# A pair of column blocks with two groups of seven products: the left block's last k group ahead of both groups in place of between them

## The chip, the cores and the metric

The kernel runs on one core of one Trainium2 chip. The metric is device time in microseconds (us) of one execution. TensorE (PE in the profile) multiplies, VectorE (DVE) and ScalarE (ACT) work element by element, GpSimd (POOL) and SyncE (SP) issue transfers here.

## The reference, cut to what matters

A decoder trunk of two layers on 256 tokens of width 2048, all in float32. Each layer has a mixer (Mamba-2 in the first, attention with forget gates in the second) and then a gated feed-forward part:

```python
def swiglu(h, w_gate_up, w_down):
    g, u = jnp.split(h @ w_gate_up, 2, axis=-1)
    return (jax.nn.silu(g) * u) @ w_down
```

The change touches `h @ w_gate_up`: 256 x 2048 by 2048 x 11264, once in each layer.

## The kernel before

**Products.** Every weight matrix is streamed once through the chip in units of 128 x 1024 numbers (512 KB: two slices of k by 512 columns). Each unit is split in two parts of lower precision: ACT casts it (`whi`, line 273), DVE subtracts the cast from the original (`wlo`, line 279). The activations are held split in the same way (`xT`, or `xS` for sums of them). A product is then the three matmuls xh*hi, xh*lo and xl*hi, added up in PSUM. An ordinary unit takes 12 matmuls (lines 554 to 556), since there are two blocks of 128 tokens.

**Pairs.** Columns are worked on in blocks of 512. `pair` takes two blocks at once: in the gate/up stage (`ffn_up`) the left one is a block of the gate matrix, the right one the same block of the up matrix. k is cut in four k groups (0 to 3). For the k groups in `crossed` the left and right weights, two by two, are multiplied by a scheme with seven products in place of eight, called f, d, c, a, e, g, b in the order in which they run (`Cross.ORDER`). Such a group (`Group`) loads five units: f, d and g are units of the weights, c and a are sums of two units, made in DRAM in advance (`next_sum`: a copy issued by SP, then an adding transfer issued by POOL). Each product takes six matmuls (lines 466 to 469). Products e and b need further sums of weights: behind the split of c, DVE adds unit d to unit c in place (line 428), and that is what e splits; behind the split of e it adds unit g, and that is what b splits.

In 9 of the 11 pairs of each layer's gate/up stage `crossed` is (1, 2), so two groups stand in one pair, and `adjacent` is true; the first and the last pair have one group. No other stage has neighbouring k groups in `crossed`, so the change concerns 18 pairs. In this text the units of a pair are L0a, L0b (left block, k group 0), R0a, R0b (right block), L3a, L3b, R3a, R3b (k group 3), the products of the first group f to b, and those of the second f' to b'.

**Who runs ahead of whom.** `stream` writes all work out in order. ACT and DVE split four pieces (units or products) ahead of the matmuls (`SPL`), into pools of four `whi` and four `wlo` buffers: the split of a piece can begin when PE is done with the piece four places before it. Units are loaded by SP into a pool of six `wraw` buffers (`RAW`); a load waits until the buffer's earlier unit has been read for the last time. What follows a pair's matmuls (silu, gating, turning the result for the next stage) is written by `Flow` between the pieces. The turning of the last pair's result takes eight matmuls against an identity matrix (line 588) and two DVE instructions (`xT<-mis`); they stand behind R0b of the next pair.

Of the kernel before, what the change touches and what calls it, by code (L numbers as in the profile page):

```python
# [232 lines left out]
def kernel(ctx: ExitStack, tc: tile.TileContext, xT_d, x_d, cols_d, rows_d, wdt_d, win_d,  # L233
# [86 lines left out]
    def halves(b, kg, src, ks):  # L320
        w = src.rearrange("p (k n) -> p k n", n=NB)
        return [Unit(b, kg, w[:, 2 * i:2 * i + 2], NB, ks[i]) for i in range(2)]
# [14 lines left out]
    def pair(xs, sources, done, fills, crossed, parts):  # L337


        both = [Block(xs, d, f) for d, f in zip(done, fills)]  # L340
        x = Cross(*both, parts)
        order, rights = [], []
        adjacent = len(crossed) > 1 and crossed[-1] == crossed[-2] + 1
        for kg in range(len(xs)):
            us = [halves(b, kg, src[kg], ([0, 2], [1, 3])) for b, src in zip(both, sources)]
            if kg in crossed:
                if not (adjacent and kg == crossed[-1]):
                    order += rights
                    rights = []
                (b11, b21), (b12, b22) = us  # L350
                c, a = Sum(b22.src, b12.src), Sum(b22.src, b21.src)
                sums.extend((c, a))
                first = {"f": b12, "d": b21, "c": Unit(None, kg, c, NB, [1, 3]),
                         "a": Unit(None, kg, a, NB, [1, 3]), "g": b11}
                order.append(Group(x, first, xs[kg], kg == crossed[0], kg == crossed[-1]))
            else:
                for b, u in zip(both, us):
                    b.units += u
                order += us[0]
                rights += us[1]  # L360
        if adjacent:

            n = next(i for i in range(len(order) - 1, 0, -1) if isinstance(order[i], Group))
            both[0].after = order.pop(n)
            order.append(both[0].after)
        blocks.append(order + rights)

    def next_sum():
# [327 lines left out]
    def out_stage(xs, w_d, wcol, crossed, summed=()):  # L696

        ss = const.tile([P, NT, 4], F32, name=nm("ss"))
        nxt = [Slot(j in summed) for j in range(4)]
        r = [None]  # L700

        def done(j):
            def run(ps):
                for t in range(NT):
                    hb = h[:, t, j * NB:(j + 1) * NB]
                    yield tt(hb, hb, ps[t])
                yield EVAC
                nxt[j].task = spawn(take(j), flow.mid)
            return run

        def take(j):
            yield SYNC
            yield from h_slot(nxt[j], j, wcol)
            for t in range(NT):
                sumsq(h[:, t, j * NB:(j + 1) * NB], ss[:, t, j:j + 1])
                yield A(0.6)
            if j == 3:
                tot = tiny(NT, "tot")
                nc.vector.tensor_reduce(out=tot, in_=ss, axis=AX.X, op=ALU.add)
                r[0] = rsqrt_of(tot, DM, NT)  # L720

        for j in (0, 2):
            pair(xs, w_d[j:j + 2], (done(j), done(j + 1)), nxt[j:j + 2], crossed, parts_to_h(j))
        return nxt, r

    def ffn_up(xs, r, gu_d, summed):
# [41 lines left out]
        for nb in range(NFB):  # L768
            x = [None]

            def took(y, x=x):
                x[0] = y
                return parts(y)

            pair(xs, gu_d[2 * nb:2 * nb + 2], (lambda ps, x=x: gate(x[0], ps), lambda ps, x=x, nb=nb: up(x[0], ps, nb)),
                 (None, acts[nb]), (1, 2) if 0 < nb < NFB - 1 else (2,), took)
# [515 lines left out]
    for j in (0, 2):  # L1292
        pair(act1, dn1_d[j:j + 2], (final(j), final(j + 1)), (None, None), DN1, parts_to_h(j))
# [104 lines left out]
```

## Time and profile before

| what | us |
|---|---|
| median of 3 runs | 2487.26 (2486.73 to 2488.52) |
| the profiled execution, own time | 2488.41 |
| its span, first to last instruction | 2486.6 |
| PE busy | 2477.7 |
| DVE busy | 1973.2 |
| ACT busy | 1435.0 |

The profiled execution's time is 1.15 above the median of the runs shown, inside their spread; 1.8 of it lies outside the span. Instructions overlap a little in the records, and a matmul's record (0.39) is longer than the distance to the next one (0.23), so a busy PE is read by the starts of its matmuls.

### The profile page before, as it was taken

Reading aid. Unit: us, or ns where it says so; the run is one execution under the profiler, and the core shown is the slowest. Engines: PE = TensorE matmul, PEld = TensorE weight load, DVE = VectorE, ACT = ScalarE, POOL = GpSimd, SP = SyncE. Lnnn points to the kernel's source line nnn. Section 1 sums busy time; section 2 is a strip of 40 time slices with the busy share of each in tenths; the row PEclk is TensorE's granted clock in tenths of the full one; section 3 lists DMA queues with packets and bytes.
Section 4 is the critical chain, followed back from the end, with each engine's and each line's share of the span. In section 5 each row is a group of like instructions: output and inputs, shape, how many; then the busy total and the mean of one; then the engine's idle time right before and its main releaser. Section 6 shows DMA issues by size and latency. Waiting matters only on the chain.

```text
span 2486.6 us, 31889 instructions
## 1 busy us (share of the span) xinstructions
PE 2477.7 (100%) x11446; PEld 2056.6 (83%) x11446; DVE 1973.2 (79%) x2557; ACT 1435.0 (58%) x1807; POOL 133.6 (5%) x168
## 2 busy tenths in 40 slices
PE   9999999999999999999999999999999999999999
PEld 8888888888888888888888888888888888888787
DVE  6677777778688999997766657678889999988867
ACT  6665566555555656564545556565565656555544
POOL 0000000000000000000000011010000000000000
PEclk9999999999999999999999999999999999999999
DMA  7887868778887988887888888676889898988765
GB/s 253 261 251 230 256 212 253 220 236 276 276 257 258 296 260 296 258 293 248 263 271 256 260 238 249 208 221 209 262 254 299 285 300 271 286 251 260 244 226 184
DMA packets 173599, 633.34 MB, mean 255 GB/s; under 512 B 19424, under 2 KB 20592, under 8 KB 171904
## 3 DMA queue, kind: packets, MB, share of 16 engines
q1 hardware_dynamic: 154656, 559.50, 64.4%
q0 software_dynamic: 18208, 71.39, 15.8%
q8 instruction: 90, 1.47, 0.2%
q14 instruction: 69, 0.57, 0.1%
q10 hardware_dynamic: 576, 0.40, 0.1%
HBM read 629.04 MB, written 123.81 MB: 303 GB/s over the span
## 4 chain that ended last, share of the span: by engine, by line
PE 98%; DVE 1%; ACT 1%; issue 0%; DMA 0%; ACTq 0%; DVEq 0%
PE acc L554 24%; PE acc L556 24%; PE acc L555 23%; PE mis L466 4%; PE mis L469 4%; PE mis L467 4%; PE acc L467 3%; PE acc L469 3%; PE acc L466 3%; PE mis L588 1%; PE mis L1027 1%; DVE wlo L279 1%; PE mis L897 0%; ACT whi L273 0%; DVE wraw L428 0%; PE mis L1033 0%
## 5 line engine op out<-in xcount | busy, mean ns | idle before, releaser
L279 DVE TENSOR_TENSOR wlo<-wraw,whi 128x1024 fp32r<-128x1024 f32 (+1 forms) x959 | 1147.5, 1219 | 306.3 <-ACT whi L273 298.0
L273 ACT CAST whi<-wraw 128x1024 fp32r<-128x1024 f32 (+1 forms) x962 | 989.1, 1049 | 671.6 <-PE acc L556 456.3
L554 PE MATMUL acc<-whi,xT 128*128 128x512 f32 x2496 | 982.0, 393 | 0.4 <-ACT whi L273 0.3
L556 PE MATMUL acc<-whi,xT 128*128 128x512 f32 x2496 | 973.1, 390 | 0.0
L555 PE MATMUL acc<-wlo,xT 128*128 128x512 f32 x2496 | 972.7, 390 | 0.0
L556 PEld LDWEIGHTS acc<-whi,xT 128*128 128x128 f32 x2496 | 469.0, 188 | 98.6
L554 PEld LDWEIGHTS acc<-whi,xT 128*128 128x128 f32 x2496 | 469.3, 188 | 97.3 <-issue 1.6
L555 PEld LDWEIGHTS acc<-wlo,xT 128*128 128x128 f32 x2496 | 469.4, 188 | 96.1 <-DVE wlo L279 1.2
L281 DVE SCALAR_TENSOR_TENSOR wlo<-wraw,cols,whi 128x512 fp32r<-128x512 f32 x192 | 134.7, 748 | 72.0 <-ACT whi L275 71.6
L275 ACT ACTIVATE whi<-wraw,cols 128x512 fp32r<-128x512 f32 x192 | 127.6, 717 | 72.2 <-PE acc L556 55.1
L428 DVE TENSOR_TENSOR wraw<-wraw,wraw 128x1024 f32<-128x1024 f32 x116 | 142.1, 1225 | 4.0
L467 PE MATMUL mis<-wlo,xS 128*128 128x512 f32 x348 | 135.5, 389 | 0.4 <-DVE wlo L279 0.4
L466 PE MATMUL mis<-whi,xS 128*128 128x512 f32 x348 | 135.4, 389 | 0.0
L469 PE MATMUL mis<-whi,xS 128*128 128x512 f32 x348 | 135.4, 389 | 0.0
L377 POOL DMA_DIRECT2D wsum<-in_gu_dram x80 | 66.3, 829 | 1026.9 <-DMA wsum<-in_gu_dram 1011.0
L467 PE MATMUL acc<-wlo,xT 128*128 128x512 f32 x224 | 87.6, 391 | 1.8 <-DVE wlo L279 1.8
L466 PE MATMUL acc<-whi,xT 128*128 128x512 f32 x224 | 87.2, 389 | 0.0
L469 PE MATMUL acc<-whi,xT 128*128 128x512 f32 x224 | 87.2, 389 | 0.0
L467 PEld LDWEIGHTS mis<-wlo,xS 128*128 128x128 f32 x348 | 65.3, 188 | 14.5 <-DVE wlo L279 0.9
L466 PEld LDWEIGHTS mis<-whi,xS 128*128 128x128 f32 x348 | 65.3, 188 | 13.6
L469 PEld LDWEIGHTS mis<-whi,xS 128*128 128x128 f32 x348 | 65.3, 188 | 13.5
L273 ACT CAST xT<-mis 128x512 fp32r<-128x512 f32 x52 | 27.9, 589 | 54.5 <-PE mis L588 52.4
(250 smaller groups left out, 2109.2 us busy)
## 6 DMA issues: line engine op xcount, KB each, us to landing
wraw<-in_gu_dram SPq DMA_DIRECT2D x312, 512.0 KB, 6.4
wraw<-in_dn_dram SPq DMA_DIRECT2D x164, 512.0 KB, 5.6
wraw<-in_win_dram SPq DMA_DIRECT2D x159, 512.0 KB, 5.9
wraw<-wsum SPq DMA_DIRECT2D x116, 512.0 KB, 5.9
wsum<-in_gu_dram SPq DMA_DIRECT2D x80, 512.0 KB, 6.8
wsum<-in_gu_dram POOLq DMA_DIRECT2D x80, 512.0 KB, 8.8
wraw<-in_wout_dram SPq DMA_DIRECT2D x60, 512.0 KB, 6.3
wraw<-in_wq_dram SPq DMA_DIRECT2D x32, 512.0 KB, 5.8
```

What stands on the lines that cost most here:

```text
L273: nc.scalar.copy(out=hi, in_=src)
L275: nc.scalar.activation(hi, src, AF.Copy, scale=scal)
L279: nc.vector.tensor_tensor(out=lo, in0=src, in1=hi.bitcast(F32), op=ALU.subtract)
L281: nc.vector.scalar_tensor_tensor(out=lo, in0=src, scalar=scal, in1=hi.bitcast(F32), op0=ALU.mult, op1=ALU.subtract)
L377: nc.gpsimd.dma_start(out=old.tile, in_=old.other, accum_op=ALU.add)
L428: nc.vector.tensor_tensor(out=us[out].raw, in0=us[in0].raw, in1=us[in1].raw, op=ALU.add)
L466: nc.tensor.matmul(ps, lhsT=xh, rhs=hi[:, p, :], start=group.first and p == 0 and name not in own, stop=False)
L467: nc.tensor.matmul(ps, lhsT=xh, rhs=lo[:, p, :], start=False, stop=False)
L469: nc.tensor.matmul(ps, lhsT=xl, rhs=hi[:, p, :], start=False, stop=stop and p == 1)
L554: nc.tensor.matmul(b.ps[t], lhsT=xh, rhs=hi[:, j, :], start=u is b.units[0] and ks[j] == 0, stop=False)
L555: nc.tensor.matmul(b.ps[t], lhsT=xh, rhs=lo[:, j, :], start=False, stop=False)
L556: nc.tensor.matmul(b.ps[t], lhsT=xl, rhs=hi[:, j, :], start=False, stop=last and j == len(ks) - 1)
```

## The change

In `pair`, when the two groups are neighbours: before, the last group was taken out and put behind the left block's last k group, which gave L0 R0 *group* L3 *group'* R3. Now all units come first and both groups behind them: L0 R0 L3 *group* *group'* R3. `after`, the group that ends the left block, is the second group in both.

```diff
         if adjacent:
 
-            n = next(i for i in range(len(order) - 1, 0, -1) if isinstance(order[i], Group))
-            both[0].after = order.pop(n)
-            order.append(both[0].after)
+            order = [u for u in order if isinstance(u, Unit)] + [u for u in order if isinstance(u, Group)]
+            both[0].after = order[-1]
         blocks.append(order + rights)
```

The new file has one line less, so lines behind it have a number lower by one.

On PE the change shows where the first group ends. Before, in a pair of the first layer, the second half of product b (`acc_7761`) and the first half unit of L3a behind it:

```order
L466 MATMUL acc_7761<-whi_7881,xT_5282 128x512
L467 MATMUL acc_7761<-wlo_7882,xT_5282 128x512
L469 MATMUL acc_7761<-whi_7881,xT_5282 128x512
L554 MATMUL acc_7760<-whi_7901,xT_6099 128x512
L555 MATMUL acc_7760<-wlo_7902,xT_6099 128x512
L556 MATMUL acc_7760<-whi_7901,xT_6099 128x512
```

In the changed kernel the same place of the same pair, with the first half of f' behind b:

```order
L465 MATMUL acc_7761<-whi_7917,xT_5282 128x512
L466 MATMUL acc_7761<-wlo_7918,xT_5282 128x512
L468 MATMUL acc_7761<-whi_7917,xT_5282 128x512
L465 MATMUL acc_7802<-whi_7937,xS_5991 128x512
L466 MATMUL acc_7802<-wlo_7938,xS_5991 128x512
L468 MATMUL acc_7802<-whi_7937,xS_5991 128x512
```

The 24 matmuls of L3a and L3b have moved from between the groups to ahead of the first one.

On DVE, before, from product e on: e, the sum for b, g, b, L3a, L3b, f', d', c', the sum for e', a' (`wlo` is a split, `wraw<-wraw,wraw` a sum of weights):

```order
L279 TENSOR_TENSOR wlo_7859<-wraw_7704,whi_7858 128x1024
L428 TENSOR_TENSOR wraw_7704<-wraw_7704,wraw_7738 128x1024
L279 TENSOR_TENSOR wlo_7871<-wraw_7738,whi_7870 128x1024
L279 TENSOR_TENSOR wlo_7882<-wraw_7704,whi_7881 128x1024
L279 TENSOR_TENSOR wlo_7902<-wraw_7758,whi_7901 128x1024
L279 TENSOR_TENSOR wlo_7915<-wraw_7779,whi_7914 128x1024
L279 TENSOR_TENSOR wlo_7927<-wraw_7819,whi_7926 128x1024
L279 TENSOR_TENSOR wlo_7939<-wraw_7885,whi_7938 128x1024
L279 TENSOR_TENSOR wlo_7955<-wraw_7887,whi_7954 128x1024
L428 TENSOR_TENSOR wraw_7887<-wraw_7887,wraw_7885 128x1024
L279 TENSOR_TENSOR wlo_7974<-wraw_7892,whi_7973 128x1024
```

In the changed kernel from the same product on: e, the sum for b, g, b, f', d', c', the sum for e', a', e', the sum for b', g':

```order
L279 TENSOR_TENSOR wlo_7895<-wraw_7738,whi_7894 128x1024
L427 TENSOR_TENSOR wraw_7738<-wraw_7738,wraw_7779 128x1024
L279 TENSOR_TENSOR wlo_7907<-wraw_7779,whi_7906 128x1024
L279 TENSOR_TENSOR wlo_7918<-wraw_7738,whi_7917 128x1024
L279 TENSOR_TENSOR wlo_7938<-wraw_7800,whi_7937 128x1024
L279 TENSOR_TENSOR wlo_7951<-wraw_7820,whi_7950 128x1024
L279 TENSOR_TENSOR wlo_7961<-wraw_7870,whi_7960 128x1024
L427 TENSOR_TENSOR wraw_7870<-wraw_7870,wraw_7820 128x1024
L279 TENSOR_TENSOR wlo_7974<-wraw_7924,whi_7973 128x1024
L279 TENSOR_TENSOR wlo_7984<-wraw_7870,whi_7983 128x1024
L427 TENSOR_TENSOR wraw_7870<-wraw_7870,wraw_7926 128x1024
L279 TENSOR_TENSOR wlo_7995<-wraw_7926,whi_7994 128x1024
```

The two splits of L3 have gone from between b and f' to ahead of f, and nothing else stands between e and g'.

## Rows read from the trace of the kernel before

**Rows 1.** The page: busy time by engine, and the chain that ended last.

```profile
PE 2477.7 (100%) x11446; PEld 2056.6 (83%) x11446; DVE 1973.2 (79%) x2557; ACT 1435.0 (58%) x1807; POOL 133.6 (5%) x168
...
PE 98%; DVE 1%; ACT 1%; issue 0%; DMA 0%; ACTq 0%; DVEq 0%
```

**Rows 2.** Busy us by stretch: nine pairs in each layer; clock, DMA share, GB/s.

```profile
733.00:1109.00 376.00, 376.00 (x1697) 312.04 (x1696) 341.70 (x340) 224.83 (x241) 14.67 (x18) 1.00 0.85 277
1825.00:2201.00 376.00, 376.00 (x1697) 312.06 (x1696) 341.67 (x341) 226.75 (x245) 17.10 (x21) 1.00 0.90 286
```

**Rows 3.** Waits of PE, whole span: total us, times, longest.

```profile
PE acc L467 <- DVE wlo L279: 1.8, 3, 0.6
```

**Rows 4.** Timeline of PE: f', d', and R3a of one pair begin.

```profile
851.61 0.39 PE L466 MATMUL acc<-whi,xS 128*128 128x512 f32 x1
851.84 0.39 PE L467 MATMUL acc<-wlo,xS 128*128 128x512 f32 x1
...
852.75 0.39 PE L469 MATMUL acc<-whi,xS 128*128 128x512 f32 x1
...
861.13 0.39 PE L554 MATMUL acc<-whi,xT 128*128 128x512 f32 x1
```

**Rows 5.** Timeline of DVE, same pair, and six splits of the next one.

```profile
850.18 1.22 DVE L279 TENSOR_TENSOR wlo<-wraw,whi 128x1024 fp32r<-128x1024 f32 x1 [1.14 <-ACT whi L273]
851.44 1.23 DVE L428 TENSOR_TENSOR wraw<-wraw,wraw 128x1024 f32<-128x1024 f32 x1
...
854.30 1.23 DVE L279 TENSOR_TENSOR wlo<-wraw,whi 128x1024 fp32r<-128x1024 f32 x1 [0.18 <-ACT whi L273]
855.56 1.23 DVE L428 TENSOR_TENSOR wraw<-wraw,wraw 128x1024 f32<-128x1024 f32 x1
856.71 3.64 DVE L279 TENSOR_TENSOR wlo<-wraw,whi 128x1024 fp32r<-128x1024 f32 x3
...
861.59 2.35 DVE L279 TENSOR_TENSOR wlo<-wraw,whi 128x1024 fp32r<-128x1024 f32 x2
...
883.70 7.04 DVE L279 TENSOR_TENSOR wlo<-wraw,whi 128x1024 fp32r<-128x1024 f32 x6
```

**Rows 6.** Timeline of ACT in the same second group.

```profile
853.22 1.06 ACT L273 CAST whi<-wraw 128x1024 fp32r<-128x1024 f32 x1 [0.35 <-PE acc L469]
854.58 1.06 ACT L273 CAST whi<-wraw 128x1024 fp32r<-128x1024 f32 x1 [0.30 <-PE mis L469]
856.90 2.00 ACT L273 CAST whi<-wraw 128x1024 fp32r<-128x1024 f32 x2 [1.27 <-DVE wraw L428]
```

**Rows 7.** Timeline of DVE and PE in the group of the layer's first pair.

```profile
720.57 1.23 DVE L279 TENSOR_TENSOR wlo<-wraw,whi 128x1024 fp32r<-128x1024 f32 x1 [0.50 <-ACT whi L273]
721.83 1.22 DVE L428 TENSOR_TENSOR wraw<-wraw,wraw 128x1024 f32<-128x1024 f32 x1
722.97 2.50 DVE L279 TENSOR_TENSOR wlo<-wraw,whi 128x1024 fp32r<-128x1024 f32 x2
725.51 1.23 DVE L428 TENSOR_TENSOR wraw<-wraw,wraw 128x1024 f32<-128x1024 f32 x1
...
726.97 0.39 PE L466 MATMUL acc<-whi,xT 128*128 128x512 f32 x1
727.92 0.50 PE L467 MATMUL acc<-wlo,xT 128*128 128x512 f32 x1 [0.56 <-DVE wlo L279]
...
728.26 0.39 PE L469 MATMUL acc<-whi,xT 128*128 128x512 f32 x1
```

**Rows 8.** Loads (line 397) from issue to landing: 852:855, 877:882, 1825:2201.

```profile
DMA to landing us min/median/max: 6.2/6.3/6.4
...
DMA to landing us min/median/max: 3.9/4.0/4.1
...
DMA to landing us min/median/max: 3.3/6.5/9.8
```

## The prediction

> **What bounds the kernel now.** I read the page first: PE is busy for 2477.7 us of 2486.6, and the chain that ended last runs over PE for 98% of the span [rows 1]. So time is saved only where PE stands still, and lost wherever something new makes it stand still. Then I cut out the nine pairs with two groups of each layer. PE is busy for 376.00 of 376.00 us in both stretches, at the full clock, and DVE for 341.7, which is 91% [rows 2]. Over the whole span PE waited only three times for a split, 1.8 us in all [rows 3]. In these 18 pairs there is nothing to win on PE, and DVE, which makes half of each split, is close behind it.
>
> The timelines of one pair show how close. PE starts f' at 851.61 and R3a, 42 matmuls later, at 861.13 [rows 4]: 9.52 us for a group, 1.36 for a product, 0.227 for a matmul. DVE has nine instructions in a group, seven splits and two sums, each of 1.22 us; where nothing is waited for it starts the next one 1.13 after the last (two splits take 2.35) [rows 5]. Nine times 1.13 is 10.2, and the waits for ACT between them come on top. Inside a group DVE is slower than PE. With an ordinary unit it is the other way round: 1.13 against the 2.72 of 12 matmuls. So a group uses up DVE's lead, and ordinary units give it back.
>
> The lead cannot be large. In the second group the cast of e starts at 853.22, released by PE [rows 6]: the last matmul of f began at 852.75 and takes 0.39 [rows 4]. That is the pool of four buffers: e takes that of f. DVE follows at 854.30 [rows 5].
>
> **The change, worked out.** No instruction is added or taken away; what counts is the distance. Before, L3a and L3b, 5.44 us of PE's time, lay between the groups and took 2.3 us of DVE's, so DVE won 3 us back. Now f' comes straight behind b. The rows of the second group before serve for the first group after, because both follow L3a and L3b and have the same instructions in the same order. I count on that pair's clock, f starting at 851.61.
>
> The first group does not wait. Its tightest product is g: its split starts at 856.71 and ends at 857.93 [rows 5]; the split's low part is read by the second matmul of g, at 851.61 + 5 x 1.36 + 0.23 = 858.64. There is 0.71 to spare.
>
> Next DVE goes straight on. The run of three splits from 856.71 is g, b and the piece behind it [rows 5], now f': it starts 3.64 - 1.22 = 2.42 after g, at 859.13. Then d' and c' at 1.13 each: 860.26 and 861.39. ACT is not in the way: b and f' are cast by 858.90 [rows 6], d' follows at once, and c' needs PE to be done with g, at 858.41 + 5 x 0.227 + 0.39 = 859.93, so its cast ends at about 861.0.
>
> From c' on the trace has the very sequence, in the only group of the layer's first pair, where DVE was late for another reason: split of c at 720.57, sum, a, e (whose cast waits for the sum), sum, g, and PE's second matmul of g starts at 727.92 after a wait on DVE [rows 7]. That is 7.35 us. So g' can go on at 861.39 + 7.35 = 868.74. Without a wait PE would be there at 851.61 + 12 x 1.36 + 0.23 = 868.16. It stands still for 0.58. The matmul behind the awaited one came 0.34 after it in place of 0.23 [rows 7], another 0.11. Together 0.69 us for each pair.
>
> What is late next is little. b' is split 1.28 after g' (its cast waits for the sum; the run of three is 1.28 + 1.14 + 1.22) while PE comes to its second matmul 1.47 after that of g', so it is in time by some 0.2. R3a and R3b then give DVE 2.72 each, and the work behind a pair (silu, gating, the turning) is written into that stretch and the next units as before. The turning's two DVE instructions now stand between the splits of f and d, in the time of L3a, which covers them.
>
> The loads move too. SP's queue has the same issues in another order, and the sums needed for the first group are asked for two units later, which helps. In the closest place, unit c' takes the buffer that the first sum of the group sets free, at 851.44 + 1.23 = 852.67 [rows 5]. Its cast may begin as late as 861.39 - 1.06 = 860.33 without cost, an allowance of 7.7 us. Two loads issued in just that place took 6.2 and 6.4, two issued into a quieter queue 3.9 and 4.1, and the stretch in layer 2 has a median of 6.5 and a longest of 9.8 [rows 8]. Unit g' goes out when g is split, at 857.93, and is first needed by the sum for b', at 861.39 + (725.51 - 720.57) = 866.33: 8.4 us. I take both as hidden, cost nothing; the upper bound is 9.8 - 7.7 = 2.1 us in a pair.
>
> The sum is 18 x 0.69 = 12.4 us, all of it added. The profiled execution took 2488.41, so 2500.8 beside it; against the median of the runs, 2487.26, this gives 2499.7, and I say 2500.
>
> One rule speaks for more. The row of six splits in a run takes 7.04 [rows 5], where six times 1.22 is 7.32: DVE's records overlap. The Trainium skill, page "VectorE: DVE Perf Modes", section "The DRAIN you can't avoid", has it that the next Vector instruction does not start before the pipeline of the last one is empty; read strictly, with the records as the time in the pipeline, there is no such overlap. By that rule the spacing is the record. In the run from e to g' six starts follow at about 1.13 to 1.14 (g, f', d', c', a', g'), and 0.085 more for each makes 0.51 more per pair, 21.6 us in all. I go by the row.
>
> **The rivals.**
> - *DVE is in time after all (not slower).* The place is g' again. The wait is 0.58 over a run of twelve DVE instructions from e to g'; if each took 0.03 less, or c' were split 0.3 earlier, less than 5 us would be lost in all, and from 0.58 on nothing. For it: the margin is small against 14.4 us of counted work. Against it: every step is a measured distance, and the start of the run is tied to PE by the buffer of f, so no lead can be saved up. Time 2487 to 2492.
> - *Loads become the bound.* Two groups back to back use ten units in 19 us, and the sums' copies and adding transfers share the DMA engines, which are 85 to 90% busy [rows 2]. If a third of the pairs paid the upper bound of 2.1, that is 6 x 2.1 = 12.6 more: 2512. Against it: the six ordinary units ahead of the groups now stand together, and their loads come at PE's pace of 2.72, so the queue should be short when c' is asked for.
> - *DVE's spacing stretches to its records.* 18 x (0.69 + 0.51) = 21.6: 2509. The row of six speaks against it.
> - *Faster.* PE would have to stand still somewhere that the change closes. All its waits on splits are 1.8 us [rows 3], and none lies in the stretches of the 18 pairs [rows 2]. Some 2485 at best, and only by an effect on another stage.
>
> **How the numbers follow.** My forecast 0.72; in time after all 0.12; loads 0.08; stretched spacing 0.05; faster 0.03. A change of 0.2%, 5 us, is about what a measurement of this kernel can tell from none. My own case has a small tail below 0.28 per pair, so: faster 0.04, same 0.13, slower 0.83. My own case alone runs from 2494 (0.4 per pair) to 2505 (1.0 per pair). The range goes on to 2491 at the low end, which takes in a part of the first rival, and to 2509 at the high end, for the stretched spacing and a few late loads.
>
> **What the new profile would show.** Some 18 more waits of PE on DVE's split, each of about 0.5 us, at the second matmul of product g' (line 466 there). The nine pairs of a layer take about 6.2 us longer in each layer, and all other stages the same. DVE runs without idle time from e to b' and idles more in the L and R units. ACT's casts wait for no loads in the groups. The prediction is wrong if PE shows no waits there, if it waits at c' or a' behind casts that wait for DMA, if it waits for PSUM banks at L0 of the next pair, or if the granted clock leaves 1.00.

## The result and the profile after

The changed kernel takes 2507.56 us (median of 4 runs, 2505.58 to 2509.13), the kernel before 2486.99 beside it (4 runs, 2486.03 to 2488.52). The ratio is 1.0079, 95% interval 1.0067 to 1.0091: 20.6 us slower, where 2500.0 was forecast. The profiled execution of the changed kernel took 2505.58, with a span of 2503.8; it is the fastest of the four, so the trace shows some 2 us less than the median.

The page of the changed kernel, busy time and the chain that ended last, against [rows 1]:

```profile
PE 2485.1 (99%) x11446; PEld 2053.5 (82%) x11446; DVE 1973.3 (79%) x2557; ACT 1437.4 (57%) x1807; POOL 133.9 (5%) x168
...
PE 84%; DVE 10%; ACT 3%; issue 2%; DMA 1%; ACTq 0%; DVEq 0%
```

DVE's work is the same to 0.1 us, yet it now holds 10% of the chain, where it held 1%. Two stretches as long as nine pairs (clock, DMA share and GB/s at the end), against [rows 2]. As there, each begins and ends some 9 us ahead of the pairs themselves, so the wait at the last pair's g' lies at its end and is not in it in full:

```profile
732.00:1116.00 384.00, 379.89 (x1694) 310.24 (x1693) 339.81 (x339) 224.91 (x240) 14.70 (x18) 1.00 0.84 268
1832.00:2217.00 385.00, 380.14 (x1698) 311.01 (x1697) 341.21 (x340) 226.10 (x242) 17.12 (x21) 1.00 0.87 279
```

The clock is still 1.00. PE now stands still in both stretches. Its waits over the whole span (total us, times, longest), against [rows 3]:

```profile
PE acc L466 <- DVE wlo L279: 9.6, 21, 0.6
...
PE acc L553 <- DVE u L675: 1.1, 2, 0.7
...
PE acc L554 <- DVE wlo L279: 0.4, 1, 0.4
```

There are 18 more waits in the groups than before, and two new kinds. One pair shows all three. Its f starts at 843.34. The timeline of PE, from g' to R3a (lines 553 to 555), and then the place in the next pair's R0a where the second token block's bank is first written:

```profile
859.66 0.39 PE L465 MATMUL acc<-whi,xT 128*128 128x512 f32 x1
860.47 0.50 PE L466 MATMUL acc<-wlo,xT 128*128 128x512 f32 x1 [0.43 <-DVE wlo L279]
860.81 0.40 PE L468 MATMUL acc<-whi,xT 128*128 128x512 f32 x1
...
863.13 0.40 PE L553 MATMUL acc<-whi,xT 128*128 128x512 f32 x1
863.91 0.50 PE L554 MATMUL acc<-wlo,xT 128*128 128x512 f32 x1 [0.39 <-DVE wlo L279]
...
875.16 0.39 PE L555 MATMUL acc<-whi,xT 128*128 128x512 f32 x1
875.64 0.50 PE L553 MATMUL acc<-whi,xT 128*128 128x512 f32 x1
```

The lengths are read from the starts, as the bracket counts only from the end of a record that overlaps. At g' the distance is 0.81 in place of 0.23, the next one 0.34: 0.70 us lost. At R3a it is 0.78, at the bank 0.47.

The timeline of DVE in the same pair: g, b, f', d', c' (the five), a sum, a' and e', a sum, g' and b', then R3a; and the read-out of the right block's second bank:

```profile
848.43 5.91 DVE L279 TENSOR_TENSOR wlo<-wraw,whi 128x1024 fp32r<-128x1024 f32 x5
854.37 1.22 DVE L427 TENSOR_TENSOR wraw<-wraw,wraw 128x1024 f32<-128x1024 f32 x1
855.51 2.51 DVE L279 TENSOR_TENSOR wlo<-wraw,whi 128x1024 fp32r<-128x1024 f32 x2
858.06 1.22 DVE L427 TENSOR_TENSOR wraw<-wraw,wraw 128x1024 f32<-128x1024 f32 x1
859.20 2.50 DVE L279 TENSOR_TENSOR wlo<-wraw,whi 128x1024 fp32r<-128x1024 f32 x2
862.63 1.23 DVE L279 TENSOR_TENSOR wlo<-wraw,whi 128x1024 fp32r<-128x1024 f32 x1 [0.93 <-ACT whi L273]
...
874.90 0.68 DVE L675 TENSOR_TENSOR u<-acc,u 128x512 f32<-128x512 f32 x1
```

From 848.43 to 861.70 DVE never stops for longer than 0.06: g' starts at once when the sum ahead of it is done, and its end, 860.42, is what PE waits for. R3a is another matter: there DVE had been idle for 0.93 and waited for ACT's cast. The timeline of ACT, that cast:

```profile
861.55 1.05 ACT L273 CAST whi<-wraw 128x1024 fp32r<-128x1024 f32 x1 [1.11 <-DMA wraw<-in_gu_dram]
```

It waited for the load of R3a. The timeline of POOL shows what was issued 0.1 us ahead of that load:

```profile
850.86 0.82 POOL L376 DMA_DIRECT2D wsum<-in_gu_dram  x1 [21.30 <-DMA wsum<-in_gu_dram]
```

The loads issued between 849.6 and 852.9, from issue to landing, are those of g' (849.68), R3a (850.96) and R3b (852.10):

```profile
DMA to landing us min/median/max: 4.2/10.5/10.6
```

The adding transfer itself took 10.8 and landed at 861.64; the load of R3a landed at 861.45. Without the wait at R3a, PE would have come to the low part 0.55 earlier, so a landing by 860.9 would have done.

At the bank, `u<-acc,u` ends at 875.58 and PE, at 875.64, comes 0.25 later than its step from 875.16 would bring it. It is read here as the rest of the same delay, since DVE's work on the finished blocks is written between the splits and came late with them; banks_freed_early puts that to the test.

The lengths of the 18 pairs, from the starts of the pairs' transposes (eight matmuls in each), worked out from the trace:

```
layer   before           after
1       41.69 to 41.73   42.50 43.05 43.53 42.49 43.03 42.53 42.51 42.49 42.44
2       41.69 to 41.74   42.52 42.49 42.53 42.51 43.15 42.49 42.53 43.47 42.42
```

Thirteen pairs are longer by 0.7 to 0.85, five by 1.3 to 1.8. The wait at g' (start distance 0.81 to 0.83) is in all 18: 18 x 0.70 = 12.6 us. The five long pairs have 3.7 more, (43.05 + 43.53 + 43.03 + 43.15 + 43.47) - 5 x 42.5. About 0.1 in each pair is left, 1.7 in all. The sum, 18.0, is 0.8 more than the spans differ by (17.2).

Most of what the long pairs lose is lost at the bank. In the three of layer 1, R3a costs 0.21, 0.66 and 0.19, and the bank 0.37, 0.36 and 0.36. In the two of layer 2, R3a's load is in time; the late one is that of the next pair's R0a (issued at 2045.50 and 2173.66, landed within 0.25 of an adding transfer), and the whole loss, 0.70 and 0.97, is at the bank. The larger one in the timeline of PE:

```profile
2187.68 0.40 PE L555 MATMUL acc<-whi,xT 128*128 128x512 f32 x1
2188.78 0.50 PE L553 MATMUL acc<-whi,xT 128*128 128x512 f32 x1 [0.69 <-DVE u L675]
```

Together that is 1.1 at R3a and 2.8 at the bank (the sum is a little over 3.7, as a plain pair also loses some 0.05 at the bank).

### The profile page after: what moved, and what is told of

The parts are those of the page before. It is cut to its first block, busy times and chain, and to the rows that moved or that the text cites. A ratio compares the mean times of both kernels' runs of the same rounds, so it can differ in the third digit from the quotient of the medians.

```text
span 2503.8 us, 31862 instructions
## 1 busy us (share of the span) xinstructions
PE 2485.1 (99%) x11446; PEld 2053.5 (82%) x11446; DVE 1973.3 (79%) x2557; ACT 1437.4 (57%) x1807; POOL 133.9 (5%) x168
## 4 chain that ended last, share of the span: by engine, by line
PE 84%; DVE 10%; ACT 3%; issue 2%; DMA 1%; ACTq 0%; DVEq 0%
PE acc L553 23%; PE acc L555 23%; PE acc L554 23%; DVE wlo L279 6%; DVE wraw L427 3%; ACT whi L273 3%; PE acc L466 2%; PE acc L468 2%; PE acc L465 2%; PE mis L587 1%; PE mis L465 1%; PE mis L468 1%; PE mis L466 1%; PE mis L1026 1%; DMA wraw<-in_gu_dram 1%
## 5 line engine op out<-in xcount | busy, mean ns | idle before, releaser
L554 PEld LDWEIGHTS acc<-wlo,xT 128*128 128x128 f32 x2496 | 469.4, 188 | 96.2 <-DVE wlo L279 2.4
L468 PEld LDWEIGHTS mis<-whi,xS 128*128 128x128 f32 x348 | 65.3, 188 | 13.5
L466 PEld LDWEIGHTS acc<-wlo,xT 128*128 128x128 f32 x224 | 42.0, 188 | 26.9 <-DVE wlo L279 18.4
```

The costliest lines, as they stand in the source:

```text
L466: nc.tensor.matmul(ps, lhsT=xh, rhs=lo[:, p, :], start=False, stop=False)
L468: nc.tensor.matmul(ps, lhsT=xl, rhs=hi[:, p, :], start=False, stop=stop and p == 1)
L554: nc.tensor.matmul(b.ps[t], lhsT=xh, rhs=lo[:, j, :], start=False, stop=False)
```

## The experiments

What the expectations call theory 1 is that the loss has separate causes: DVE's lag at g', in every pair, and late loads behind the second group, in some (and, once the rows above had been read for it, the banks of the next block). The rivals have it that one cause carries the whole, or that the causes need each other. All edits but one are to the changed kernel.

**One ordinary unit between the groups (half_between).** L3b goes back between the groups, L3a stays ahead of them.

```diff
-            order = [u for u in order if isinstance(u, Unit)] + [u for u in order if isinstance(u, Group)]
+            units, groups = [u for u in order if isinstance(u, Unit)], [u for u in order if isinstance(u, Group)]
+            order = units[:-1] + groups[:1] + units[-1:] + groups[1:]
```

> Order L0 R0 L3a group L3b group' R3: one of the two units put back between the groups. Theory 1 (DVE falls behind in two groups in a row): one ordinary unit gives DVE 2.72 - 1.13 = 1.6 us back, more than the 0.58 by which g' was late, so PE does not wait at g' and the time is that of before, 2487, within 3 us. Theory 2 (loads bound the two groups, or the unit order as such): the loads are still asked for in nearly the changed order and the late ones behind the second group stay, 2493 to 2503.

Measured: 2490.0 (10 runs) against 2487.63 (25 runs), ratio 1.0009, interval 1.0000 to 1.0018. PE waits at no g', and in layer 1 it is busy throughout a stretch as long as nine pairs:

```profile
733.00:1109.00 376.00, 376.00 (x1696) 312.02 (x1695) 341.80 (x340) 227.32 (x241) 14.70 (x18) 1.00 0.86 276
```

Pairs are 41.69 to 41.79 long, but for one of 42.29 and one of 41.89. A single ordinary unit, 12 matmuls and one split, is enough: it gives DVE 2.72 - 1.13 = 1.59 back, more than the 0.58 that it lacked. So distance between the groups takes the wait away; whether a unit other than L3b would do as well was not tried.

**The second group's last sum left out (no_second_sum).** The addition of unit g' to the sum, ahead of the split of b', is left out, so b' is not the product that it should be. One DVE instruction of 1.14 less stands ahead of g'.

```diff
-        if name in late:
+        second = group.cross.left.after is group
+        if name in late and not (second and name == "e"):
             add(*late[name])
```

> The changed kernel without the second group's sum for b' (b' splits the weights that e' split): one DVE instruction of 1.22 us less between e' and g'. Theory 1: DVE is 1.13 us earlier at g', which was late by 0.58, so none of the 18 waits at g' stays and 12.6 us come back; late loads at R3a may stay: 2488 to 2495. Theory 2 (loads): the same loads at the same time, PE waits for casts that wait for DMA, 2500 or more.

Measured: 2492.75 (10 runs, 2489.54 to 2495.61), ratio 1.0019, interval 1.0009 to 1.0028. The waits of PE fall back in the groups, and those at R3a stay:

```profile
PE acc L467 <- DVE wlo L279: 1.8, 3, 0.6
...
PE acc L555 <- DVE wlo L279: 1.3, 3, 0.8
```

In layer 1 five pairs are 41.69 to 41.82 long, the other four 42.06, 42.35, 43.16 and 42.21. So 5.1 us are left with no wait at g' at all, and they are in single pairs, in layer 1 at R3a.

**No adding transfers (no_adding_transfers).** POOL's adding transfers of the gate/up stages are left out, so the sums for c and a are only copies.

```diff
         if old is not None:
-            nc.gpsimd.dma_start(out=old.tile, in_=old.other, accum_op=ALU.add)
+            if not old.alone:
+                nc.gpsimd.dma_start(out=old.tile, in_=old.other, accum_op=ALU.add)
...
                 c, a = Sum(b22.src, b12.src), Sum(b22.src, b21.src)
+                c.alone = a.alone = gu
```

> The changed kernel without the adding transfers of the gate/up stages (the sums c and a are only copies of their first unit). Theory 1: all 18 waits at g' stay, 0.70 us each, 12.6 us; only the waits behind the second group, at R3a and at the next R0, go, since their loads no longer run beside an adding transfer: 2499 to 2501. Theory 2 (loads bound it): back to 2487 to 2491.

Measured: 2502.56 (4 runs), ratio 1.0060, interval 1.0045 to 1.0075, above the 2499 to 2501 of theory 1. All 18 waits at g' are there. One of them in the timeline of PE:

```profile
818.02 0.50 PE L468 MATMUL acc<-wlo,xT 128*128 128x512 f32 x1 [0.44 <-DVE wlo L279]
```

All nine pairs of layer 1 are 42.51 to 42.55. In layer 2 seven are 42.45 to 42.53 and two are longer, 42.83 and 43.77. The longest lies where the adding transfers for the down stage, which this kernel keeps, have begun: five loads issued beside one of these at 2130.3, which took 9.9, took 8.1 to 9.35. (In layer 1 such transfers run too, and there no pair is longer.) So the long pairs of layer 1 go with the adding transfers, and the wait at g' does not.

**Both left out (neither).** The two edits together.

> Both left out: the sum for b' and the adding transfers. Theory 1 with the late loads as its second part: no wait is left in the pairs, 2487 within 2 us. If a third cause is at work (banks, SP's queue), some 3 us or more over 2487 stay.

Measured: 2487.27 (10 runs), ratio 0.9999, interval 0.9989 to 1.0008. PE is busy throughout this stretch of layer 1:

```profile
732.00:1109.00 377.00, 377.00 (x1702) 312.94 (x1701) 331.55 (x332) 225.73 (x240) 4.98 (x6) 1.00 0.78 258
```

The two costs add up: 14.9 without adding transfers, 5.1 without the second sum, 20.0 together, against 20.6 for the change. With both taken away nothing is left that these times can show. In the pairs PE still waits twice, for 0.3 at R3a of layer 1's last pair (1111.0) and for 0.5 in layer 2 (2088.3).

**The same sum left out of the kernel before (before_no_sum).** The edit of no_second_sum, made to the kernel before, as a control.

> The kernel before without the second group's sum for b'. Theory 1: PE stands still nowhere in these pairs, so DVE's time is worth nothing there: the same as before, 2487, within 2 us. If leaving a sum out were a gain by itself, by some 10 us as in the changed kernel, the reading of those runs would fall.

Measured: 2487.39 (10 runs) against 2487.15 (13 runs), ratio 1.0001, interval 0.9991 to 1.0010. Less DVE work is worth nothing where PE does not wait for it, so what no_second_sum won came from the wait.

**The first group's sum left out (no_first_sum).** The same addition, of unit g for b, but in the first group of a pair. This tells whether DVE can carry a lead from one group to the next.

```diff
-        if name in late:
+        first = group.first and not group.last and group.cross.left.after is not None
+        if name in late and not (first and name == "e"):
             add(*late[name])
```

> The changed kernel without the first group's sum for b (b splits the weights that e split). The same one DVE instruction less between the first e and g' as in the run without the second group's sum, but ahead of c'. Theory 1 (the lead is capped by the four buffers): ACT may not cast c' before PE is done with g, 859.93 on the clock of the prediction, so the split of c' begins at 861.05 in place of 861.39 and only 0.34 of the 1.13 counts: PE still waits at g', 0.24 + 0.11 = 0.35 us in each pair in place of 0.70, pairs of 42.1 to 42.2 us in place of 42.5, and about 6 us less than the changed kernel in all. Rival (DVE's sum of work over both groups decides): as without the second sum, no wait at g' and pairs of 41.7.

Measured: 2499.35 (4 runs), ratio 1.0051, interval 1.0036 to 1.0066. The timeline of PE, one of the 18 waits at g':

```profile
815.58 0.39 PE L466 MATMUL acc<-whi,xT 128*128 128x512 f32 x1
816.07 0.50 PE L467 MATMUL acc<-wlo,xT 128*128 128x512 f32 x1
```

The timeline of ACT, three of the casts in the first group ahead of it:

```profile
803.60 1.06 ACT L273 CAST whi<-wraw 128x1024 fp32r<-128x1024 f32 x1 [0.32 <-PE mis L469]
804.90 1.06 ACT L273 CAST whi<-wraw 128x1024 fp32r<-128x1024 f32 x1 [0.25 <-PE mis L469]
806.26 1.06 ACT L273 CAST whi<-wraw 128x1024 fp32r<-128x1024 f32 x1 [0.30 <-PE mis L469]
```

The distance at g' is 0.48 or 0.49 in 17 of the 18 pairs (in one, where PE had already stood still for 0.8 at a split of the same group, 0.92): 0.25 late, and 0.11 for the next matmul, 0.36 in place of 0.70. DVE was spared 1.14 us, and got 0.34 of it. The rest went into waiting for buffers: each cast is released by PE, at 1.36 us, the pace of the products. So the pool of four is the limit of the lead, as the prediction said. Two numbers missed what was expected. The pairs of layer 1 are 42.30 (the last 42.12), not 42.1 to 42.2, since in eight of them PE stops at R0a's second bank too, where it loses 0.17. And the time is 8.2 below the changed kernel, not about 6; layer 1 has no long pair here.

**The sums asked for elsewhere (sums_shifted).** In layer 1 the copies and adding transfers, which go out at every ninth load, do so four loads earlier, to take the adding transfer away from R3a's load.

```diff
-                if pace and i % pace == pace - 1:
+                if pace and i % pace == (4 if 224 <= i < 440 else pace - 1):
                     next_sum()
```

> The changed kernel with the copies and adding transfers of layer 1's gate/up stage asked for five units earlier or four later (ahead of L0b and g in place of L3b and a'), nothing left out. Theory 1 with late loads as its second part: the adding transfer is over when R3a is loaded, so layer 1's nine pairs all take 42.5 us, the waits at g' stay, and the total is 1 to 3 us below the changed kernel. If the late loads have another cause, layer 1 keeps pairs of 43 us and more.

Measured: 2506.73 (4 runs), ratio 1.0080, interval 1.0065 to 1.0095; the expectation of nine pairs of 42.5 failed. Layer 1 has pairs of 43.86, 43.41 and 43.27, the others 42.44 to 42.53. The timeline of ACT, a cast that waited:

```profile
830.16 1.05 ACT L273 CAST whi<-wraw 128x1024 fp32r<-128x1024 f32 x1 [2.68 <-DMA wraw<-in_gu_dram]
```

Its load, issued at 820.01, from issue to landing:

```profile
DMA to landing us min/median/max: 10.1/10.1/10.1
```

The waits of PE for banks, over the whole span:

```profile
PE acc L553 <- DVE u L675: 4.5, 6, 1.1
```

The adding transfer, 819.8 to 830.2, now lies beside the loads a little further on, and these are late instead. No wait at R3a is left in layer 1, and the long pairs lose their time at the bank. So the late loads moved with the adding transfer; what fell is the thought that four loads earlier there is a free place.

**The banks freed early (banks_freed_early).** The two additions that read the right block's banks are written one behind the other, with no split between them.

```diff
-            for t in range(NT):
-                yield tt(s[t], ps[t], s[t])
+            yield tt(s[0], ps[0], s[0]) + tt(s[1], ps[1], s[1])
```

> The changed kernel with the two DVE instructions that empty the right block's banks written next to each other, so that the second one (u<-acc,u) comes one split, 1.14 us, earlier; nothing left out. Theory: behind the second group DVE is late (by itself, and more where R3a's or R3b's load is late), and PE feels it where the next pair's R0a needs the right block's second bank. If so, these bank waits go, the waits at g' stay: pairs of 42.4 to 42.5, about 3 to 5 us less than the changed kernel, 2501 to 2504. If the late loads cost at the splits of R3a and R3b themselves, nothing changes, 2506 to 2508.

Measured: 2504.57 (5 runs, 2500.92 to 2506.05) against 2487.39 (21 runs), ratio 1.0066, interval 1.0053 to 1.0078. This is 17.2 over before, where the change is 20.6 over, and between the two times expected. The plain pairs are 42.41 to 42.47, and the small step at the second bank of R0a is gone; the longest are 43.23 and 42.81. Late loads still make PE wait at R3a, as one row of its timeline shows:

```profile
861.86 0.50 PE L554 MATMUL acc<-wlo,xT 128*128 128x512 f32 x1 [0.48 <-DVE wlo L279]
```

So the banks are worth some 3 us, by a median of runs that spread by 5; that agrees with the 2.8 counted at the bank above. The trace is of the fastest run, 3.7 below the median.

**One unit between, again, and with the banks freed early (half_and_banks, half_banks_early).** half_and_banks is half_between once more, and half_banks_early has both edits.

> Placeholder of the same order as half_between, once more, beside the next one, to see whether its 2.4 us over before stay: 2488 to 2491.

> L3a ahead, L3b between the groups, and the banks freed early as in the first of these runs. Theory: neither g' nor the banks are waited for, 2487 within 1.5 us, 1 to 3 us below the same order without it.

Measured, each with 11 runs: 2488.61, ratio 1.0005, interval 0.9996 to 1.0013; and 2487.73, ratio 1.0002, interval 0.9993 to 1.0011. Neither can be told from before, nor, at 0.9 apart, from each other; the 2.4 us of half_between did not come again. In half_banks_early one pair of layer 2 is 42.37, with a wait at g' that was not expected. No version was found that beats it; with PE busy all through these pairs [rows 2], none of these could.

**The wait at g' alone (only_g).** All adding transfers are left out, in every stage, so the sums are only copies, and the banks are freed early.

> The changed kernel with two things taken away at once: every adding transfer of the sums is left out (in the gate/up, down and attention stages, so the checksum rows are not what the reference has), and the second evacuation of a block's banks stands right behind the first. Theory 1 (three separate causes: the wait at g', 18 x 0.70 = 12.6 us; the loads beside adding transfers; the banks of the next block): only the first is left, so the start distance at g' is 0.81 to 0.83 in all 18 pairs, every pair is 42.40 long, and the time is 2487.4 + 12.6 = 2500, within 1 us. Rival (a fourth cause that the others hid, or the wait at g' needs the late loads in part): pairs of differing length, or 2503 and more, or 2496 and less.

Measured: 2500.2 (4 runs) against 2486.66 (7 runs), ratio 1.0056, interval 1.0039 to 1.0073. All 18 pairs are 42.47 long, and PE's waits in the groups are what they were:

```profile
PE acc L468 <- DVE wlo L279: 9.6, 21, 0.6
```

Of the 13.5 us that are left, 18 x 0.70 = 12.6 is the wait at g'. The pairs have 0.07 more than expected. The starts between the waits are 0.2271 apart on average (in the changed kernel too), against 0.2268 before, which makes 0.06 in 180 matmuls; why is open.

Deeper buffers, which might let DVE save up a lead or the loads go out earlier, were not tried.

## Why the prediction was right in its sign and low in its size

**The wait at g' was right, place and size.** Counted from the start of f, the split of c' came at 853.12 - 843.34 = 9.78, forecast 9.78 (861.39 - 851.61). PE's second matmul of g' came at 860.47 - 843.34 = 17.13, forecast 17.13. The wait and the late matmul behind it cost 0.59 + 0.11, forecast 0.58 + 0.11. Some 18 more waits, at line 466, were foretold, and 18 came. only_g, which has little else, took 2500.2, where the forecast for the whole was 2500.0.

**Its reasons held.** Distance gives the lead back (half_between), the pool of four caps it (no_first_sum), and b' was in time. The first group did not wait at g: its split starts at 848.43, 5.09 behind f, as forecast (856.71 - 851.61 = 5.10).

**The step that failed is the loads.** Of 20.6 us, 12.6 is the wait that was forecast; late loads and what hangs on them were priced at nothing and took some 5 (2507.56 - 2502.56); the rest is the 0.1 in each pair and what these times leave open. The prediction looked at the units c' and g', took "both as hidden, cost nothing", and so they were: that of g' landed after 4.2. It went no further along the queue. R3a's and R3b's loads go out next, 1.3 and 2.4 behind that of g', and in layer 2 R0a's is late; the sentence "R3a and R3b then give DVE 2.72 each" takes their data for granted. By the pair shown they had 9.9 us (850.96 to 860.9) and took 10.5 beside an adding transfer. The landings in [rows 8], up to 9.8, already said that 9.9 is no safe allowance, and the first layer of the kernel before has slower ones. There, two loads issued at 993.9 and 995.0, beside an adding transfer issued at 993.2, took from issue to landing:

```profile
DMA to landing us min/median/max: 10.0/10.0/10.1
```

The adding transfer took 10.6.

Before, such loads cost PE nothing. The adding transfers of layer 1's nine pairs got somewhat slower by the change (8.9 on average before, 9.5 after; the longest 10.6 and 10.8). What changed more is which loads run beside them, and the slack. In the pair of [rows 4] R3a's load went out at 846.79, 2.5 ahead of the adding transfer, and landed at 854.09, 3.8 before its cast; in the changed kernel it goes out within 0.4 of an adding transfer in all nine pairs of layer 1. And two groups take in ten units in 19 us and leave DVE with no lead at R3a. There R3a's load took 10.0 to 10.5 in the three long pairs and 7.9 to 9.3 in the other six, so the 9.9 is where it begins to cost. The rival "loads become the bound" priced 12.6 on top of the wait at g', for c', with upper bound 2.1 and a third of the pairs; the loads that did come late were others, and most of what they cost was paid at the bank.

**The banks were overlooked.** Among its signs of being wrong the prediction named a wait for banks at L0 of the next pair; it came, but at R0a, whose second bank is read by `u<-acc,u` only after another split. The margin there was 0.25 before the change (u's record ended at 872.44, PE came at 872.69). A late R3a pushes all of DVE's work behind it, and PE pays a second time at the bank: 43.53 in the pair shown is 1.0 over a plain one, of which 0.66 arose at R3a and 0.36 at the bank.

**The rivals.** DVE was not in time. Nothing was won elsewhere. The price of the first one had a slip: with c' split 0.3 earlier 0.28 of the wait is left, and with the 0.11 behind it 18 x 0.39 = 7.0 us, not less than 5; no_first_sum, 0.34 earlier, had 0.36 a pair. The stretched spacing did not come either: five splits run in 5.91 us, where five records of 1.22 are 6.1, and this five holds one stop of 0.05. The Trainium skill, page "VectorE: DVE Perf Modes", section "The DRAIN you can't avoid", has the next instruction wait for an empty pipeline, but adds that one that is not held starts earlier. The prediction took up only the first half; starts of 1.13 to 1.14 apart with records of 1.22 fit the second. The range, 2491 to 2509, held the time because of its room for a few late loads and for the stretched spacing, of which the second never came; that is luck in part. The likeliest case's own range, up to 2505, did not hold it.

## What to carry to other kernels

When work is moved closer together, follow each queue past the last piece that is moved: check every load up to the next place where the engines have slack, against the slowest landing in the trace and not its median. Two pieces that each use up an engine's lead need one between them that gives it back, and here a single ordinary unit was enough. Where a buffer pool caps the lead, work saved early is mostly lost (0.34 of 1.14 us here), while the same work saved right ahead of the wait took all of it away (0.59).

## What the runs showed of the hardware that was not expected

- Loads issued right beside an adding transfer (512 KB, from DRAM to DRAM) land about when it lands: 10.5 and 10.6 us beside one of 10.8, 10.1 beside one of 10.5, 10.0 and 10.1 beside one of 10.6 in the kernel before; the other loads within 15 us of the pair shown took 3.4 to 8.5. In nine pairs of layer 1 all 29 loads issued within 2.5 us behind one landed from 0.9 before it to 1.5 after it; in layer 2 some landed up to 3.2 before it. Moving the adding transfer moved the late loads with it.
- A matmul that starts after a wait has a record of 0.50 in place of 0.39, and the next one starts 0.34 behind it, not 0.23. A wait thus costs 0.11 us more than it lasts, at g', at R3a and at the bank alike.
